# A two-layer encoder trunk on one core: output passes that start on half of their input, pools and allocations in another order, a norm on four columns

## The chip, the cores and the metric

The kernel runs on one core of a Trainium2 chip. The metric is device time in microseconds (us) of one execution; before the change the median of 3 runs is 1994.59 us (1993.06 to 1995.67). TensorE is PE here (its weight loads PEld), VectorE is DVE, ScalarE ACT, GpSimd POOL, and SP is the engine whose queue issues nearly all DMAs.

## The reference, cut to what matters

512 tokens of width 2048, all in float32. Layer A is a gated pooling mixer, then a key/value side is computed once, then layer B is latent attention.

```python
def pool_mixer_layer(x, norm_g, w_in, w_group, scale, w_out):      # layer A
    proj = rmsnorm(x, norm_g) @ w_in                  # 2048 -> 8192
    u, gate = proj[..., :W_A], proj[..., W_A:]        # 4096 each
    u = u.reshape(B, S, 4, 1024)                      # 4 groups, windows 2, 4, 8, 16
    pooled = stack([causal_mean_pool(u[:, :, g], w) - u[:, :, g] for g, w in ...])
    y = einsum('bsgc,gcd->bsgd', pooled, w_group) * scale
    return x + (y * silu(gate)) @ w_out               # 4096 -> 2048
...
h = rmsnorm(x, kv_norm_g); ckv = h @ kv_w_a; c = rmsnorm(c, kv_latent_g)   # shared k, v
...
proj = rmsnorm(x, norm_g) @ w_in                      # layer B: 512 latent + 2048 gate
q = rmsnorm(q_lat, q_latent_g) @ w_q_b                # 16 heads of 192
x + (attention(q, k, v) * silu(gate)) @ w_out
```

## The kernel before, in words

Activations lie with the feature on the partition and the 512 tokens along the row. A float32 product is three matmuls on rounded halves: hi times hi, hi times lo, lo times hi. "hi" is a cast on ACT, "lo" the difference, on DVE.

**Layer A, first pass (lines 384 to 431).** The 64 tiles of 128 columns of `awin` are made in 32 pairs. Each pair is computed by a seven-product scheme: for each of four quarters `q`, `w_combos` (269) loads 2 x 256 KB of weights into `raw`, DVE makes two sums (274), POOL two more (276, 277), ACT casts seven combinations to `hi` (280), DVE subtracts to `lo` (281). `seven` (291) then issues 21 matmuls of 256 columns for each of the two input blocks `j` of the quarter. A pair is 168 matmuls. `gather` (304) adds the pieces from PSUM. Pairs 0 to 15 are pooled (`pool_pair`, 318: log2(w) shifted adds, then a scale and a subtraction, then a store to `raws` in DRAM); pairs 16 to 31 are gates (`silu_pair`). The tuple `late` (402) is the order of the pairs. The norm of x is computed once in this pass (`norm_r`, 165): a matmul with a matrix of ones sums over the partitions, and the Newton steps of `rsqrt` (156) run on 128x512.

**Layer A, groups and output passes (433 to 487).** For b = 0 and 1: `group(2b, 0)` and `group(2b+1, 4)` multiply pooled groups by `awg`, eight accumulators each, all eight PSUM banks. At its end DVE multiplies each accumulator by scale and gate (457), then sums (463 to 465), ACT and DVE split them into the blocks `xh[j], xl[j]`: j = 0 to 3 from the first group, 4 to 7 from the second. The output pass then makes eight pairs of `awo`, each over q = 0 to 3, that is over j = 0 to 7 in order; b = 0 adds x, b = 1 adds the result of b = 0, and stores to `xres`.

**Layer B.** The pools of layer A are closed, and rpool, wpool, apool, bpool, xpool and tpool3 are opened in their place, at addresses in that order, from the lowest up. Each x tile is read back from `xres` (506), cast with the norm's gain (153, 154), and multiplied with `wkvc` into five accumulators. Then `norm_r` makes 1/rms of x, and DVE multiplies the accumulators by it (563, 566). Four latents (`proj` on `bwin`), two `latent_norm`, 16 gates, then eight units of two heads of attention, and the output projection.

A scheduler puts the instructions of each engine in order, and each engine runs its own list in that order; SP's list of DMAs too. A tile of a new pool waits for the last use of what lay at its address.

Of the kernel before, what the change touches and what calls it, by code (L numbers as in the profile page):

```python
# [51 lines left out]
def trunk_kernel(  # L52
# [111 lines left out]

    def norm_r(acc, n, p=None, r=None):

        p = tr() if p is None else p
        T.matmul(p, ones, acc, start=True, stop=True)
        v, a = (t[:, 0, 0:S] for t in (pt(), pt())) if r is not None else (tt_(), tt_())
        r = rpool.tile([P, S], F32, tag="r", name="r") if r is None else r  # L170
        V.tensor_scalar(v, p, 1.0 / n, EPS, ALU.mult, ALU.add)
        rsqrt(v, r, a, S)
        return r

# [59 lines left out]
    with ExitStack() as c1:  # L234
# [82 lines left out]

        def pool_pair(pair, v):

            w = WINS[pair // 4]  # L320
            up = pt()
            G.memset(up[:, :, 0:PAD], 0.0)
            V.tensor_tensor(halves(up[:, :, PAD:]), v, halves(r2), ALU.mult)
            prev, off = up, PAD
            m = 1
            while m < w:
                ext = w - 2 * m
                nw = S + ext
                nx = pt()
                V.tensor_tensor(nx[:, :, 0:nw], prev[:, :, off - ext:off + S],  # L330
                                prev[:, :, off - ext - m:off + S - m], ALU.add)
                prev, off = nx, ext
                m *= 2
# [67 lines left out]
        early = (18, 19, 20, 21)  # L401
        late = (22, 0, 23, 1, 2, 24, 3, 12, 25, 13, 26, 14, 27, 15, 28, 8, 29, 9, 30, 10, 11, 4, 5, 6, 7, 31)
        for n, pair in enumerate(early + late):
# [8 lines left out]
            if n == 4:  # L412
                V.tensor_tensor(sq[:, 0, :], sq[:, 0, :], sq[:, 1, :], ALU.add)
                p = ps7.tile([P, 2, H], F32, tag="k3", name="k3").rearrange("p h t -> p (h t)")
                norm_r(sq[:, 0, :], D, p, r2[:, 0, :])
                V.tensor_scalar(r2[:, 1, :], r2[:, 0, :], -1.0, None, ALU.mult)
            v = gather(ks)
            if n < 4:
                raws[pair] = dram()
                for m in range(2):  # L420
                    nc.sync.dma_start(raws[pair][:, m, :].rearrange("p (h t) -> p h t", h=2), v[:, m])
            elif pair < 16:
                pool_pair(pair, v)
                if pair < 6:
                    finish_gates(16 + pair)
            else:
                silu_pair(pair, halves(pt()[:, :, 0:S]), v, halves(r2))
# [4 lines left out]

        pp = c1.enter_context(tc.tile_pool(name="pp", bufs=2, **tile_))

        def group(g, j0):
# [14 lines left out]
            for o in range(8):  # L450
                if o % 2 == 0:
                    ys.append(pp.tile([P, 4, H], F32, tag="y", name="y", bufs=4))
                y = ys[-1][:, 2 - 2 * (o % 2):4 - 2 * (o % 2), :]
# [16 lines left out]
        for b in range(2):  # L470
            group(2 * b, 0)
            group(2 * b + 1, 4)
            for pair in range(NJ):
                ks = banks()
                for q in range(NJ // 2):
                    w = w_combos(*(awo[2 * b + q // 2, 2 * pair + m][:, (q % 2) * S:(q % 2 + 1) * S]
                                   for m in range(2)))
                    seven(ks, w, 2 * q)
                    seven(ks, w, 2 * q + 1)
                res = pp.tile([P, 2, S], F32, tag="y", name="y", bufs=4)  # L480
                nc.sync.dma_start(res, xres[pair] if b else xT[2 * pair:2 * pair + 2].rearrange("k p t -> p k t"))
                v = gather(ks)
                for m, op in enumerate((ALU.add, ALU.subtract)):
                    x = res[:, m, :].rearrange("p (h t) -> p h t", h=2)
                    V.tensor_tensor(x, x, v[:, m], op)
                xres[pair] = dram("xres", 16)
                nc.sync.dma_start(xres[pair], res)


    rpool = ctx.enter_context(tc.tile_pool(name="rpool", bufs=2, **tile_))  # L490
    wpool = ctx.enter_context(tc.tile_pool(name="wpool", bufs=3, **tile_))
    apool = ctx.enter_context(tc.tile_pool(name="apool", bufs=32, **tile_))
    bpool = ctx.enter_context(tc.tile_pool(name="bpool", bufs=32, **tile_))
    xpool = ctx.enter_context(tc.tile_pool(name="xpool", bufs=16, **tile_))
    tp[0] = ctx.enter_context(tc.tile_pool(name="tpool3", bufs=7, **tile_))
    ps = ctx.enter_context(tc.tile_pool(name="ps", bufs=2, space=bass.MemoryType.PSUM, **tile_))
# [46 lines left out]
    def latent_norm(lat, gcol):  # L543
        ac = tt_()
        A.activation(ac, lat[0], AF.Square)
        for o in range(1, 4):
            sq = tt_()
            A.activation(sq, lat[o], AF.Square)
            V.tensor_tensor(ac, ac, sq, ALU.add)
        r = norm_r(ac, 512)  # L550
        res = []
# [6 lines left out]

    rb[0] = norm_r(accs[0], D)
    cl = []  # L560
    for o in range(4):
        c = xt()
        V.tensor_tensor(c, kacc[o], rb[0], ALU.mult)  # L563
        cl.append(c)
    krT = tt_()
    V.tensor_tensor(krT, racc, rb[0], ALU.mult)
    pk = tr()
# [407 lines left out]
```

## Time and profile before

| | |
|---|---|
| median of 3 runs | 1994.59 us |
| the profiled execution | 1994.62 us, of which the span of the program is 1992.8 us |
| PE busy | 1914.0 us (96%) |
| PE weight loads | 1754.6 us (88%) |
| DVE busy | 1442.8 us (72%) |
| ACT busy | 848.6 us (43%) |
| POOL busy | 499.4 us (25%) |
| DMA | 254.53 MB, 128 GB/s over the span |
| mean granted clock of PE | 0.989 of full speed |

The stages of the profiled execution, in us from the start of the span: loading and first gates to about 60, the rest of the first pass to 685, groups of b = 0 to 764, its output pass to 942, groups of b = 1 to 1030, its output pass to 1212, the key/value input to 1276, latents and gates and the first unit's preparation to 1480, attention and output to 1993. PE is busy nearly throughout, so time can be lost only where PE is idle or runs at its lower clock: the view of PE's waits says for whom it waits, the timeline says when.

### The profile page before, as it was taken

To read this page: it belongs to the slowest core of one execution; us is meant where nothing else is said; L and a number is where in the kernel's file an instruction comes from. 1 tells how busy PE (TensorE), PEld (TensorE's weight loads), DVE (VectorE), ACT (ScalarE), POOL (GpSimd) and SP (SyncE) were. 2 spreads that over 40 slices of the span, in tenths; PEclk is the share of its full clock that TensorE was granted. 3 is DMA by queue.
4 is the path that set the end of the run, shared out by engine and by line. 5 is a ranking of instruction groups with operands and counts; after the bars stand their busy time and mean duration, and the time that the engine had idled before them with its cause. 6 is when DMAs were issued, how large, how long until landed. Compare 5 with 4: busy or idle time off the path is not lost.

```text
span 1992.8 us, 32684 instructions
## 1 busy us (share of the span) xinstructions
PE 1914.0 (96%) x12508; PEld 1754.6 (88%) x12508; DVE 1442.8 (72%) x2195; ACT 848.6 (43%) x1425; POOL 499.4 (25%) x516
## 2 busy tenths in 40 slices
PE   8999999999999997999998998899999999999999
PEld 7999999999999887999877997688888888888887
DVE  8779889999899867776576767674344788887322
ACT  7534333333333333333333335333243777785221
POOL 0434445555555205232033330000010111110000
PEclk9999999999999998999999998899999999999999
DMA  6644544334435563445544444222222111111632
GB/s 197 215 135 125 170 150 147 128 121 134 138 119 168 181 207 109 151 157 180 160 147 137 159 139 154 89 91 100 96 90 78 57 55 38 58 59 54 210 122 86
DMA packets 212046, 254.53 MB, mean 128 GB/s; under 512 B 14257, under 2 KB 155441, under 8 KB 211889
## 3 DMA queue, kind: packets, MB, share of 16 engines
q1 hardware_dynamic: 211600, 252.24, 39.1%
q8 instruction: 98, 1.61, 0.3%
q14 instruction: 60, 0.48, 0.1%
q10 hardware_dynamic: 288, 0.20, 0.0%
HBM read 219.88 MB, written 32.51 MB: 127 GB/s over the span
## 4 chain that ended last, share of the span: by engine, by line
PE 69%; DVE 15%; DMA 6%; issue 5%; ACT 4%; POOL 1%; SPq 1%; DVEq 0%; ACTq 0%; POOLq 0%
PE k L301 10%; PE k L299 10%; PE k L297 10%; PE mm L143 7%; PE mm L145 7%; PE mm L144 7%; DVE lo L281 5%; DMA raw<-awin 2%; PE k L143 2%; PE k L144 2%; PE k L145 2%; PE sc L766 2%; DMA raw<-awo 2%; PE mm L640 1%; PE mm L641 1%
## 5 line engine op out<-in xcount | busy, mean ns | idle before, releaser
L297 PE MATMUL k<-xh,hi 128*128 128x256 f32 x2576 | 706.0, 285 | 13.7 <-ACT xh L148 9.7
L299 PE MATMUL k<-xl,hi 128*128 128x256 f32 x2576 | 709.6, 285 | 3.2 <-DVE xl L149 3.2
L301 PE MATMUL k<-xh,lo 128*128 128x256 f32 x2576 | 648.9, 286 | 17.8 <-DVE lo L281 17.5
L280 ACT CAST hi<-raw 128x1792 fp32r<-128x1792 f32 x184 | 311.6, 1693 | 549.8 <-PE k L301 327.3
L297 PEld LDWEIGHTS k<-xh,hi 128*128 128x128 f32 x2576 | 495.3, 193 | 16.1 <-ACT xh L148 10.6
L299 PEld LDWEIGHTS k<-xl,hi 128*128 128x128 f32 x2576 | 498.2, 193 | 4.4 <-DVE xl L149 4.4
L281 DVE TENSOR_TENSOR lo<-raw,hi 128x1792 fp32r<-128x1792 f32 x184 | 405.9, 2207 | 108.2 <-ACT hi L280 107.7
L301 PEld LDWEIGHTS k<-xh,lo 128*128 128x128 f32 x2576 | 459.9, 193 | 23.1 <-DVE lo L281 22.5
L276 POOL TENSOR_TENSOR raw<-raw 128x256 f32<-128x256 f32 x184 | 218.6, 1188 | 728.6 <-DVE raw L274 656.6
L126 DVE TENSOR_TENSOR wlo<-raw,whi 128x512 fp32r<-128x512 f32 (+2 forms) x213 | 138.4, 656 | 178.3 <-ACT whi L125 177.2
L125 ACT CAST whi<-raw 128x512 fp32r<-128x512 f32 (+2 forms) x213 | 124.6, 596 | 272.0 <-PE mm L144 225.5
L277 POOL TENSOR_TENSOR raw<-raw 128x256 f32<-128x256 f32 x184 | 230.5, 1253 | 14.2
L274 DVE TENSOR_TENSOR raw<-raw 128x512 f32<-128x512 f32 x184 | 136.3, 741 | 47.0 <-DMA raw<-awo 25.5
L143 PE MATMUL mm<-bt,whi 128*128 128x512 f32 x348 | 137.5, 395 | 9.3 <-DVE xt L563 9.3
L145 PE MATMUL mm<-bt,wlo 128*128 128x512 f32 x348 | 137.0, 394 | 0.2 <-DVE wlo L126 0.2
L144 PE MATMUL mm<-bt,whi 128*128 128x512 f32 x348 | 136.5, 392 | 0.0
L144 PE MATMUL k<-lo,hi 128*128 128x512 f32 x256 | 99.6, 389 | 0.0
L145 PE MATMUL k<-hi,lo 128*128 128x512 f32 x256 | 99.6, 389 | 0.0
L149 DVE TENSOR_TENSOR lo<-raw,hi 128x1536 fp32r<-128x1536 f32 x32 | 56.0, 1756 | 54.7 <-ACT hi L148 50.8
L148 ACT CAST hi<-raw 128x1536 fp32r<-128x1536 f32 x32 | 47.2, 1482 | 96.1 <-PE k L145 60.4
L143 PEld LDWEIGHTS mm<-bt,whi 128*128 128x128 f32 x348 | 66.0, 190 | 24.2 <-issue 10.6
L145 PEld LDWEIGHTS mm<-bt,wlo 128*128 128x128 f32 x348 | 66.0, 190 | 14.7 <-DVE wlo L126 0.6
(815 smaller groups left out, 3064.1 us busy)
## 6 DMA issues: line engine op xcount, KB each, us to landing
raw<-awin SPq DMA_DIRECT2D x240, 256.0 KB, 3.2
raw<-awo SPq DMA_DIRECT2D x128, 256.0 KB, 3.1
raw<-bwin SPq DMA_DIRECT2D x80, 256.0 KB, 2.5
scr<-tp SPq DMA_DIRECT2D x32, 512.0 KB, 3.2
raw<-awg SPq DMA_DIRECT2D x32, 512.0 KB, 4.0
raw<-bwo SPq DMA_DIRECT2D x59, 256.0 KB, 2.6
raw<-scr SPq DMA_DIRECT2D x32, 256.0 KB, 4.3
y<-scr SPq DMA_DIRECT2D x32, 256.0 KB, 3.9
```

What stands on the lines that cost most here:

```text
L126: V.tensor_tensor(lo[:, :n], raw[:, :n], f(hi[:, :n]), ALU.subtract)
L143: T.matmul(dst, wh, xh, start=first, stop=False)
L144: T.matmul(dst, wh, xl, start=False, stop=False)
L145: T.matmul(dst, wl, xh, start=False, stop=last)
L274: V.tensor_tensor(c[:, :, 4:6, :], c[:, :, 0:1, :].broadcast_to([P, 2, 2, P]), c[:, :, 1:3, :], ALU.add)
L276: G.tensor_tensor(c[:, :, 6, :], c[:, :, 4, :], c[:, :, 2, :], ALU.add)
L277: G.tensor_tensor(c[:, :, 7, :], c[:, :, 6, :], c[:, :, 3, :], ALU.add)
L280: A.copy(hi, c[:, :, 1:8, :])
L281: V.tensor_tensor(lo, c[:, :, 1:8, :], f(hi), ALU.subtract)
L297: T.matmul(dst, hi[:, j % 2, wi, :], xh[j][:, xi, :], start=first, stop=False, skip_group_check=True)
L299: T.matmul(dst, hi[:, j % 2, wi, :], xl[j][:, xi, :], start=False, stop=False, skip_group_check=True)
L301: T.matmul(dst, lo[:, j % 2, wi, :], xh[j][:, xi, :], start=False, stop=last, skip_group_check=True)
```

## The change

Four parts.

1. **Output passes.** Each output pass issues quarters 0 and 1 of pairs 0 and 1 (the first group's half, j = 0 to 3) ahead of quarters 2 and 3 of pair 0. Pairs 2 to 7 are as before.
2. **Pools.** Layer B's pools are opened in the order rpool, wpool, tpool3, xpool, apool, bpool.
3. **Norm.** The sum over partitions is made with x as the weights and one column of ones as the stream, four times, so that it comes out with one token per partition, 128x4. `rsqrt` runs on 128x4. The four columns are spread on a diagonal (a 128x512 product with the identity), a matmul with ones brings them back to a row on every partition, ACT copies it out. Before the norm of layer B, ACT copies the five accumulators out of PSUM; the multiplications by 1/rms follow from there.
4. **Last group.** Pairs 12 to 15 (window 16) are only scaled and stored in the first pass, and pooled in the first output pass, after each odd pair, in `y` tiles of which there are four. The tuple `late` has another order.

```diff
+    def norm_r(acc, n, p, dg, outs):
+        for t in range(4):
+            T.matmul(p[:, t:t + 1], acc[:, t * P:(t + 1) * P], ones[:, 0:1], start=True, stop=True)
+        v, a, y = (spool.tile([P, 4], F32, tag=f"n{i}", name=f"n{i}", bufs=1) for i in range(3))
+        V.tensor_scalar(v, p[:, 0:4], 1.0 / n, EPS, ALU.mult, ALU.add)
+        rsqrt(v, y, a, 4)
+        V.tensor_tensor(dg.rearrange("p (t q) -> p t q", t=4), ident[:, None, :].broadcast_to([P, 4, P]),
+                        y[:, :, None].broadcast_to([P, 4, P]), ALU.mult)
+        T.matmul(p, ones, dg, start=True, stop=True)
+        for r, c in outs:
+            A.activation(r, p, AF.Copy, scale=c)
...
-        late = (22, 0, 23, 1, 2, 24, 3, 12, 25, 13, 26, 14, 27, 15, 28, 8, 29, 9, 30, 10, 11, 4, 5, 6, 7, 31)
+        late = (22, 0, 8, 23, 1, 9, 24, 2, 10, 25, 3, 11, 26, 4, 12, 27, 5, 13, 28, 6, 14, 29, 7, 15, 30, 31)
...
+            elif pair < 16:
+                z = pt()[:, :, 0:S]
+                V.tensor_tensor(halves(z), v, halves(r2), ALU.mult)
+                raws[pair] = dram()
+                nc.sync.dma_start(raws[pair], z)
...
+                if b == 0 and pair % 2:
+                    up = yp()
+                    nc.sync.dma_start(up[:, :, PAD:], raws[12 + pair // 2])
+                    pool_pair(12 + pair // 2, up, yp)
+            out_part(0, (0, 1))
+            out_part(1, (0, 1))
+            for pair in range(NJ):
+                out_part(pair, (2, 3) if pair < 2 else (0, 1, 2, 3))
+                out_end(pair)
...
     rpool = ctx.enter_context(tc.tile_pool(name="rpool", bufs=2, **tile_))
     wpool = ctx.enter_context(tc.tile_pool(name="wpool", bufs=3, **tile_))
+    tp[0] = ctx.enter_context(tc.tile_pool(name="tpool3", bufs=7, **tile_))
+    xpool = ctx.enter_context(tc.tile_pool(name="xpool", bufs=16, **tile_))
     apool = ctx.enter_context(tc.tile_pool(name="apool", bufs=32, **tile_))
     bpool = ctx.enter_context(tc.tile_pool(name="bpool", bufs=32, **tile_))
-    xpool = ctx.enter_context(tc.tile_pool(name="xpool", bufs=16, **tile_))
-    tp[0] = ctx.enter_context(tc.tile_pool(name="tpool3", bufs=7, **tile_))
...
-    rb[0] = norm_r(accs[0], D)
...
-        V.tensor_tensor(c, kacc[o], rb[0], ALU.mult)
+        A.copy(c, kacc[o])
         cl.append(c)
     krT = tt_()
-    V.tensor_tensor(krT, racc, rb[0], ALU.mult)
+    A.copy(krT, racc)
+    rb[0] = norm_r(accs[0], D, tr(), tt_(), [(r_tile(), 1.0)])
+    for c in cl:
+        V.tensor_tensor(c, c, rb[0], ALU.mult)
+    V.tensor_tensor(krT, krT, rb[0], ALU.mult)
```

The order of the instructions moves at these places. First, PE in the output pass of b = 0, where the second of pair 0's four weight blocks gives way to the next work. Before: after `hi_8231` (quarter 1 of pair 0) comes `hi_8283` (quarter 2 of pair 0) with `xh_8129`, the first block of the second group.

```order
L297 MATMUL k2_8171<-xh_7843,hi_8231 128x256
L299 MATMUL k2_8171<-xl_7844,hi_8231 128x256
L301 MATMUL k2_8171<-xh_7843,lo_8232 128x256
L297 MATMUL k0_8169<-xh_8129,hi_8283 128x256
L299 MATMUL k0_8169<-xl_8130,hi_8283 128x256
```

Now `hi_8251` is quarter 0 of pair 1, and `xh_7777` is a block of the first group; the second group's first block, `xh_8093`, follows 168 matmuls after the start of the pass, where it followed after 84.

```order
L308 MATMUL k2_8243<-xl_7778,hi_8251 128x256
L306 MATMUL k3_8244<-xh_7777,hi_8251 128x256
L308 MATMUL k3_8244<-xl_7778,hi_8251 128x256
L310 MATMUL k0_8133<-xh_7797,lo_8196 128x256
L310 MATMUL k1_8134<-xh_7797,lo_8196 128x256
```

Moved: two of pair 1's four weight blocks now stand ahead of the second group's half. DVE's list between the two groups' products and `xl` of the second group's second block holds five subtractions of line 281 (now 290) where it held three.

Second, SP's list at the end of the second output pass. Before, the first x tile of layer B (`tt__12418`) stands behind the store of the last pair:

```order
L487 DMA xres<-y 128x1024
L124 DMA raw<-wkvc 128x512 x3
L487 DMA xres<-y 128x1024
L506 DMA tt__12418<-xres 128x512
L124 DMA raw<-wkvc 128x512
L506 DMA tt__12472<-xres 128x512
```

Now three x tiles stand ahead of it; the first waits for PE alone (for the matmuls on the block that lay at its address):

```order
L512 DMA xres<-y 256x1x512
L542 DMA tt__12442<-xres 128x512
L124 DMA raw<-wkvc 128x512 x3
L542 DMA tt__12496<-xres 128x512
L542 DMA tt__12521<-xres 128x512
L512 DMA xres<-y 256x1x512
L124 DMA raw<-wkvc 128x512
```

Moved: three loads of 256 KB, from behind the last store to ahead of it.

Third, PE at the norm of layer B. Before, the matmul of the norm (L168), then the first latent, which waits for DVE to empty its bank:

```order
L523 MATMUL sc<-at,whi 64x512
L524 MATMUL sc<-at,whi 128x512
L168 MATMUL tr<-tt__12411,ones 128x512
L143 MATMUL mm<-bt,whi 128x512
L144 MATMUL mm<-bt,whi 128x512
```

Now four one-column matmuls, then the first latent, which waits for ACT's copy; the second matmul of the norm (L176 into `tr`) stands 40 matmuls further down.

```order
L559 MATMUL sc<-at,whi 64x512
L560 MATMUL sc<-at,whi 128x512
L170 MATMUL tr<-ones,tt__12435 128x1 x4
L143 MATMUL mm<-bt,whi 128x512
L144 MATMUL mm<-bt,whi 128x512
```

Moved: the Newton steps are no longer between the last product and the first latent on PE. From the first gate on, PE's list is as before.

## Rows read from the trace of the kernel before

**Rows 1.** Window of the first pass: length, then busy time of each engine (instructions), clock, DMA
```profile
core 0: us, PE busy (x) PEld busy (x) DVE busy (x) ACT busy (x) POOL busy (x), PEclk, DMA share, GB/s
60.00:685.00 625.00, 615.31 (x5048) 609.65 (x5047) 561.90 (x496) 236.60 (x175) 307.05 (x250) 1.00 0.46 148
```

**Rows 2.** PE's waits, whole span: us in total, times, longest us
```profile
PE k L301 <- DVE lo L281: 17.5, 20, 2.3
PE k L297 <- ACT xh L148: 9.7, 3, 5.3
```

**Rows 3.** Windows: openings (336 matmuls) of both output passes, parts, and what follows
```profile
764.50:800.40 35.90, 27.24 (x184) 25.79 (x185) 31.80 (x35) 13.78 (x12) 17.73 (x9) 0.86 0.37 119
764.50:821.10 56.60, 46.37 (x337) 44.33 (x338) 46.67 (x49) 20.81 (x17) 22.84 (x15) 0.91 0.40 128
821.10:941.90 120.80, 120.80 (x1009) 120.80 (x1009) 86.08 (x82) 42.01 (x30) 35.84 (x44) 1.00 0.51 165
1032.60:1071.00 38.40, 28.68 (x189) 27.21 (x190) 30.08 (x36) 13.69 (x12) 15.29 (x10) 0.87 0.39 123
1032.60:1091.10 58.50, 47.19 (x337) 45.12 (x338) 44.23 (x48) 20.72 (x17) 20.25 (x15) 0.91 0.38 123
```

**Rows 4.** Timeline of DVE in the openings: start, us, instruction, idle before
```profile
795.24 2.02 DVE L281 TENSOR_TENSOR lo<-raw,hi 128x1792 fp32r<-128x1792 f32 x1
...
799.16 1.22 DVE L149 TENSOR_TENSOR xl<-ts,xh 128x1024 fp32r<-128x1024 f32 x1 [1.11 <-ACT xh L148]
801.18 0.69 DVE L274 TENSOR_TENSOR raw<-raw 128x512 f32<-128x512 f32 x1 [0.80 <-DMA raw<-awo]
...
1069.80 1.22 DVE L149 TENSOR_TENSOR xl<-ts,xh 128x1024 fp32r<-128x1024 f32 x1
```

**Rows 5.** Timeline of POOL in the first opening
```profile
771.15 8.21 POOL L276 TENSOR_TENSOR raw<-raw 128x256 f32<-128x256 f32 x1 [6.08 <-DVE raw L274]
```

**Rows 6.** Timeline of all engines at the start of layer B
```profile
1212.20 0.37 ACT L308 COPY e<-k 128x256 f32<-128x256 f32 x1 [8.39 <-PE k L301]
...
1215.29 1.29 DVE L485 TENSOR_TENSOR y<-y,e 128x512 f32<-128x512 f32 x2
...
1217.03 0.38 SPq L506 DMA_DIRECT2D tt__12418<-xres  x1
...
1221.06 0.72 ACT L153 ACTIVATE at<-tt__12418,cs 128x512 fp32r<-128x512 f32 x1 [0.27 <-DMA tt__12418<-xres]
...
1221.83 1.23 PE L143 MATMUL mm<-at,xt 128*128 128x512 f32 x2 [9.67 <-ACT at L153]
```

**Rows 7.** Timeline of DVE and PE at the norm of layer B, and a window after
```profile
1276.82 0.68 DVE L171 TENSOR_SCALAR tt__12965<-tr 128x512 f32<-128x512 f32 x1
...
1285.71 0.76 PE L143 MATMUL mm<-bt,whi 128*128 128x512 f32 x1 [9.33 <-DVE xt L563]
...
1285.70:1291.60 5.90, 5.89 (x14) 4.64 (x15) 2.42 (x5) 0.62 (x1) 0.00 (x0) 0.50 0.01 3
```

**Rows 8.** Small work: a norm's weight loads, four transposes, a Newton step on eight columns
```profile
L168 PEld LDWEIGHTS tr<-tt__12411,ones x2: 188/188/189, 1275.1 to 1275.4; 128*128 128x128 f32 x2
...
1294.02 0.60 PE L569 MATMUL tr<-cs,tt__12988 128*128 128x128 f32 x4
1294.38 0.48 PE L143 MATMUL mm<-bt,whi 128*128 128x512 f32 x1
...
L163 DVE SCALAR_TENSOR_TENSOR sy<-sa,sy 128x8 f32<-128x8 f32 x22 | 4.0, 182 | 0.5
```

**Rows 9.** PE's waits from 320 to 470 (pools of window 16)
```profile
PE k L301 <- DVE lo L281: 3.1, 4, 1.0
```

**Rows 10.** PE's waits from 582 to 665 (five pools in a row)
```profile
PE k L301 <- DVE lo L281: 3.4, 4, 1.0
```

**Rows 11.** PE's waits from 240 to 300 (two pools in a row before)
```profile
PE k L301 <- DVE lo L281: 0.7, 1, 0.7
```

**Rows 12.** A group of DVE from 60 to 685: busy us, mean ns, idle before
```profile
L337 DVE SCALAR_TENSOR_TENSOR tp<-tp 128x1024 f32<-128x1024 f32 x16 | 24.3, 1517 | 0.2
```

More of the change, by code (lines that the diff above doesn't have):

```diff
@@ L163, in rsqrt, with r_tile @@
             V.scalar_tensor_tensor(y, a, 1.5, y, ALU.add, ALU.mult)
[L165 to L173, printed above, removed]
+    def norm_r(acc, n, p, dg, outs):
[9 more added lines that the diff above has]
+            A.activation(r, p, AF.Copy, scale=c)
+        return outs[0][0]
+    def r_tile():
+        return rpool.tile([P, S], F32, tag="r", name="r")
     post = const.tile([P, 4], I32, name="post")
@@ L316, in halves, with pool_pair @@
             return a.rearrange("p m (h t) -> p m h t", h=2)
-        def pool_pair(pair, v):
+        def pool_pair(pair, up, nt):
             w = WINS[pair // 4]
-            up = pt()
             G.memset(up[:, :, 0:PAD], 0.0)
-            V.tensor_tensor(halves(up[:, :, PAD:]), v, halves(r2), ALU.mult)
             prev, off = up, PAD
@@ L328, in pool_pair @@
                 nw = S + ext
-                nx = pt()
+                nx = nt()
                 V.tensor_tensor(nx[:, :, 0:nw], prev[:, :, off - ext:off + S],
@@ L414, in trunk_kernel @@
                 p = ps7.tile([P, 2, H], F32, tag="k3", name="k3").rearrange("p h t -> p (h t)")
-                norm_r(sq[:, 0, :], D, p, r2[:, 0, :])
-                V.tensor_scalar(r2[:, 1, :], r2[:, 0, :], -1.0, None, ALU.mult)
+                norm_r(sq[:, 0, :], D, p, pt()[:, 0, 0:S], [(r2[:, 0, :], 1.0), (r2[:, 1, :], -1.0)])
             v = gather(ks)
@@ L421, in trunk_kernel @@
                     nc.sync.dma_start(raws[pair][:, m, :].rearrange("p (h t) -> p h t", h=2), v[:, m])
-            elif pair < 16:
-                pool_pair(pair, v)
+            elif pair < 12:
+                up = pt()
+                V.tensor_tensor(halves(up[:, :, PAD:]), v, halves(r2), ALU.mult)
+                pool_pair(pair, up, pt)
                 if pair < 6:
                     finish_gates(16 + pair)
+            elif pair < 16:
[3 more added lines that the diff above has]
+                nc.sync.dma_start(raws[pair], z)
             else:
@@ L433, in trunk_kernel, with y_tile, yp @@
         pp = c1.enter_context(tc.tile_pool(name="pp", bufs=2, **tile_))
+        def y_tile():
+            return pp.tile([P, 2 * (PAD + S)], F32, tag="y", name="y", bufs=4)
+        def yp():
+            return y_tile().rearrange("p (m t) -> p m t", m=2)
         def group(g, j0):
@@ L451, in group @@
                 if o % 2 == 0:
-                    ys.append(pp.tile([P, 4, H], F32, tag="y", name="y", bufs=4))
+                    ys.append(y_tile()[:, 0:2 * S].rearrange("p (m t) -> p m t", m=4))
                 y = ys[-1][:, 2 - 2 * (o % 2):4 - 2 * (o % 2), :]
@@ L472, in trunk_kernel, with out_part, out_end @@
             group(2 * b + 1, 4)
-            for pair in range(NJ):
-                ks = banks()
-                for q in range(NJ // 2):
+            ks = {}
+            def out_part(pair, qs):
+                if qs[0] == 0:
+                    ks[pair] = banks()
+                for q in qs:
                     w = w_combos(*(awo[2 * b + q // 2, 2 * pair + m][:, (q % 2) * S:(q % 2 + 1) * S]
                                    for m in range(2)))
-                    seven(ks, w, 2 * q)
-                    seven(ks, w, 2 * q + 1)
-                res = pp.tile([P, 2, S], F32, tag="y", name="y", bufs=4)
+                    seven(ks[pair], w, 2 * q)
+                    seven(ks[pair], w, 2 * q + 1)
+            def out_end(pair):
+                res = yp()[:, :, 0:S]
                 nc.sync.dma_start(res, xres[pair] if b else xT[2 * pair:2 * pair + 2].rearrange("k p t -> p k t"))
-                v = gather(ks)
+                v = gather(ks.pop(pair))
                 for m, op in enumerate((ALU.add, ALU.subtract)):
@@ L549, in latent_norm @@
             V.tensor_tensor(ac, ac, sq, ALU.add)
-        r = norm_r(ac, 512)
+        r = norm_r(ac, 512, tr(), tt_(), [(r_tile(), 1.0)])
         res = []
```

## The prediction, written before the changed kernel was run

> **What bounds the kernel now.** The windows by stage come first. In the first pass PE is busy for 615.3 of 625 us at full clock [rows 1], and behind the opening of the first output pass it runs 1009 matmuls in 120.8 us without a gap, 0.12 us each [rows 3]. So PE is the bound nearly everywhere, and time can be won only where it stands still or runs slowly. PE's waits, read second, name those places: 17.5 us for the `lo` halves of DVE, 9.7 us for `xh` of ACT [rows 2]; the timelines add one stop at the start of layer B, 9.67 us, and one at its norm, 9.33 us [rows 6, 7]. The windows of the two openings, read third, are to be seen against the stretch behind them: 336 matmuls take 56.6 and 58.5 us where 336 times 0.12 is 40.3 [rows 3]. So 16.3 and 18.2 us are lost there, partly in stops, partly at a granted clock of 0.91. The profiled execution, 1994.62 us, is the base of the sum; the median of the runs, 1994.59, is the same within 0.03.
>
> **Openings of the output passes.** PE waits for the second group's blocks, which DVE and ACT make in a chain. DVE ends the last of them at 800.4 us (799.16 + 1.22) in the first opening and at 1071.0 in the second [rows 4]. Of the 336 matmuls only 184 and 189 have run by then [rows 3]; the rest take another 20.7 and 20.1 us. After the change the half of pair 1 that needs only the first group has been moved ahead, and by PE's order some 68 matmuls are left behind the last block: 8.2 us. Against that, DVE's list holds two more `lo` and three more sums ahead of that block (2 x 2.02 + 3 x 0.69 = 6.1 us, rows 4), and in the first opening also one add of a pool (1.5, the duration in rows 12): 7.6. DVE is idle for 4.1 of 35.9 us until its last block in the first opening, for 8.3 of 38.4 in the second [rows 3]. If all idle time is filled the last block is 3.5 us later in the first and no later in the second; if none, 7.6 and 6.1. Gain: 20.7 - 8.2 less 3.5 to 7.6 is 4.9 to 9.0, and 20.1 - 8.2 less 0 to 6.1 is 5.8 to 11.9. I take 8.0 and 9.5, towards the filled end, since the added work needs nothing of the second group. As outer bounds I keep nothing (the supply itself is the bound) and all that is lost, 16.3 and 18.2.
>
> **First pass.** The order of pairs changes where PE waits for `lo`. The pools of window 16 cost 3.1 us [rows 9] and five pools in a row 3.4 [rows 10]; both patterns go. In their place two pools and a gate follow each other at four places, and such a place costs 0.7 [rows 11], together 2.8; two of them have small windows, so I take 2.6. Gain 3.9; bounds 0 and 6.5.
>
> **The four last pools.** They move into the first output pass. Each is four adds and the final subtraction, 1.5 us each [rows 12], so some 7.5 us of DVE, 30 us in all. Behind the opening DVE is busy for 86.1 of 120.8 us [rows 3]; with the three pools that fall there it is about 109, 90% busy, as in the first pass, where that cost about 10 of 625 us [rows 1]. Each pool also loads 512 KB into a `y` tile on SP's queue, behind a store, and the first pool's add stands ahead of the second group's last block on DVE: if its load is late, that block is. I charge 1.5 us; bounds 0 and 6.
>
> **Start of layer B.** Before, DVE's sums of the last pair end with the add at 1215.29, then come the store, the load of x at 1217.03, ACT's cast of 0.72 at 1221.06, and PE at 1221.83 [rows 6]. PE loses 9.67 us and then, by the rate after the norm (0.42 us where 0.24 is full rate, rows 7), about 2.5 us at half clock: 12.2. Now three x tiles are loaded ahead of the last store, so that ACT can cast right behind its copy of the last pair: copy 0.37, cast 0.72 [rows 6], a square and `xt` of about 0.6 each, PE at about 1214.4. From there the first four blocks are paced by DVE, which still has gather and adds (some 4 us) in its list ahead of its `lo` halves. I leave 5 us lost: gain 7.2, bounds 2 and 10.
>
> **Norm of layer B.** The Newton chain runs from 1276.82 to PE's next matmul at 1285.71; PE stands 9.33 us, then makes 14 matmuls in 5.90 us at a granted clock of 0.50, the lower of the two levels, 1.2 GHz [rows 7]: 14 x (0.42 - 0.24) = 2.5 more. That is 11.8. After the change ACT's first copy releases the first latent's bank, and the steps on 128x4 take 11 x 0.18 = 2 us [rows 8] plus a product of 0.7; PE has 40 matmuls, 9.6 us, before the norm's second one. So PE waits for one copy at most. Gain 11.5; bounds 8 (DVE, held by its multiplications, is late with a weight half for the latents) and 11.8.
>
> **The norm's own matmuls.** A float32 matmul loads its weights twice (two loads of 0.188 us, rows 8); four one-column matmuls are eight loads, in four norms 32. Four transposes held PE for 0.36 us, 0.09 each [rows 8]. Between 0.09 and 0.188 a load this is 2.9 to 6.0 us. I take 2.9, since the transposes are the nearest whole instructions; as far as the columns hide behind other work it is less: bounds 1 and 6.
>
> **Rest.** From the first gate of layer B on, each engine has the same order; I take nothing there. The copies of the accumulators are five of ACT, some 3 us, hidden beside the first latent.
>
> **Sum.** 8.0 + 9.5 + 3.9 - 1.5 + 7.2 + 11.5 - 2.9 = 35.7 us; 1994.6 - 35.7 = 1958.9, in round figures 1959.
>
> **The rivals.** (1) The openings stay as long as they were, because what PE waits for is the supply of weight blocks and not the order. For it: POOL's sum of the third weight block took 8.21 us [rows 5], and the third block is needed after as many matmuls as before; in DVE's new list the second group's blocks stand behind `lo` halves that need POOL. Against it: the long waits for `xh` were 9.7 us of the whole span [rows 2], and they are what the new order puts off. Then 17.5 us of gain go: 1976.4. A page speaks for a milder form. The 8.21 us are longer than any single DVE instruction around them, the longest being 2.02 [rows 4]. The Trainium skill, "SBUF — State Buffer", section "Who interferes with whom", says that a DVE operation with two SBUF inputs and a POOL operation that reads SBUF exclude each other, and the loser is held until the other's instruction ends; the trace shows a hold across several instructions, not one. By the page's rule POOL would be done some 6 us sooner there and the opening less bound by supply; by the row a fuller DVE holds POOL longer. The measured row decides, and it is why I do not take the upper bound.
>
> (2) Slower. PE's stops in the openings do not go but are cut small: with work on both sides of each late block PE stops often and never long, and the clock stays at its lower level through both openings. At the rate of rows 7 (0.42 for 0.24) 336 matmuls take 70.6 us, 14.0 and 12.1 above before. Then the sum is 35.7 - 17.5 - 26.1 = -7.9: 2002.5. It decides only if the clock is low for most of the 40 us; with 0.91 before [rows 3], and fewer stops by the new order, little speaks for it. The Trainium skill, "TensorE: Matmul & The Clock Gate", section "HAM oscillation — how this bites in real kernels", says that work which comes in bursts between waits keeps dropping back to the slow clock. Here a stop of 9.33 us is followed by a clock of 0.50 [rows 7], and a mix of short stops by 0.91 [rows 3]; the trace bears it out only for the long one.
>
> (3) The change does not do what it says at the start of layer B: the loads of x, which now stand ahead in SP's list, wait for PE to leave the tiles' addresses, and weight loads stand behind them. Then the gain of 7.2 there is nothing: 1966.1.
>
> (4) The openings come near PE's own time: all 16.3 and 18.2 us come back, 17.0 more than in the sum: 1941.9.
>
> **How the numbers follow.** The forecast gets 0.58, rival 1 0.14, rival 3 0.15, rival 4 0.10, rival 2 0.03. Between the bounds of the terms the forecast reaches from about 1947 to 1972, rivals 1 and 3 lie at 1976 and 1966; from 1945 to 1977 the range leaves out rivals 4 and 2 and the forecast's edges, under 2 in 10. About 0.2%, 4 us, is what a measurement of this kernel can tell from no change; all cases but rival 2, and mishaps that add up, lie beyond it on the fast side: faster 0.94, same 0.02, slower 0.04.
>
> **What would show it.** Right: each opening's 336 matmuls take 47 to 50 us; PE's waits no longer list the casts of x in layer B and the product of the norm at over 9 us, and DVE's first x block of layer B follows the last pair's adds closely; waits for `lo` in the first pass fall by some 4 us; no stop appears in the first output pass. Wrong: openings still at 56 us or more with POOL's sums as long (rival 1); a clock under 0.7 in them (rival 2); the cast of x in layer B still behind the last store (rival 3); a new wait of PE behind a pool in the first output pass, or at the second matmul of a norm.

## The result, and the profile after

The changed kernel takes 1974.27 us (median of 4 runs, 1973.28 to 1975.29) beside 1993.82 for the kernel before (the median of 4 runs): a ratio of 0.9901, with a 95% interval of 0.9884 to 0.9918. All ratios below are times over the kernel before, with this interval in brackets. A second measurement on another occasion gave 0.9896 (0.9883 to 0.9908). It is faster by some 20 us. The forecast was 1959, the range 1945 to 1977: the sign and the range hold, the gain is a little over half of the 35.7 us in the sum. The time lies outside the forecast's own edges, 1947 to 1972, and close to the 1976.4 of rival 1, so the range held by the room that was left for the rivals.

The profiled execution has a span of 1971.5 us, 21.3 less than before. PE is busy for as long as before (1914.0 us), so what has gone is its idle time: 56.3 us where it was 78.8:

```profile
PE 1915.2 (97%) x12540; PEld 1753.3 (89%) x12540; DVE 1423.4 (72%) x2198; ACT 853.6 (43%) x1435; POOL 508.1 (26%) x516
```

PE's waits over the whole span, in us, times and longest (against [rows 2]; line 301 is now 310, 297 is 306, 281 is 290):

```profile
PE k L310 <- DVE lo L290: 13.1, 22, 1.2
...
PE k L308 <- DVE xl L149: 5.8, 3, 2.9
PE k L306 <- ACT hi L289: 4.3, 7, 0.8
PE mm L143 <- ACT xt L125: 2.1, 1, 2.1
...
PE k L306 <- ACT xh L148: 1.0, 2, 0.5
```

The stop of 9.33 us at the norm is gone, the one at the start of layer B is 2.1 where it was 9.67, and the waits for `xh` in the openings fell from 9.7 to 1.0 us. But two waits, mostly in the same openings, have taken part of their place: `xl` takes 5.8 us (3.2 before) and `hi` 4.3 (0.4 before).

Where the time went is read best by stages, cut at the first matmul of each; "layer B" starts at the end of the last matmul of the second output pass, so that its first stop lies in it. All runs of this study stand in the table (profiled execution, us); "first" reaches to the first group, "layer B" to the start of a run of 170 matmuls of the first unit's preparation that is the same in all (1486 us into the kernel before). The changed kernel stands there twice, and the two executions differ by up to 2.3 us in a stage. Other runs that share the order of every engine in a stage with it differ by more: 669.2 to 673.0 in the first pass (changed, r1, u1, u3, m1, d1), 177.6 to 181.0 in the first output pass (changed, r1, u3, n1, n2). So differences under some 3.5 us in these passes are not read. The groups of b = 1 (91.7 to 92.6 in runs with the changed order) and layer B (257.5 to 258.8 in runs with its three changes there) repeat within 1.3.

| run | first | groups b=0 | output b=0 | groups b=1 | output b=1 | layer B | rest |
|---|---|---|---|---|---|---|---|
| before | 674.7 | 89.8 | 177.5 | 90.6 | 179.5 | 273.9 | 506.8 |
| changed | 671.8 | 89.3 | 179.2 | 91.7 | 173.8 | 258.4 | 507.2 |
| changed again (r1) | 673.0 | 89.4 | 177.6 | 92.6 | 176.1 | 258.8 | 506.9 |
| u1 no early half of pair 1 | 671.2 | 89.2 | 181.2 | 92.0 | 179.1 | 258.1 | 508.0 |
| u2 pools and order undone | 679.2 | 89.6 | 173.5 | 89.3 | 175.2 | 257.6 | 507.6 |
| u3 old pool order in layer B | 670.8 | 89.2 | 181.0 | 92.0 | 176.8 | 264.5 | 507.7 |
| u4 old norm, no copies | 670.7 | 89.4 | 178.4 | 92.6 | 175.3 | 267.0 | 506.7 |
| m1 sums on DVE | 670.1 | 90.4 | 182.2 | 92.3 | 175.1 | 258.5 | 507.2 |
| m3 pools undone, new order | 678.0 | 89.4 | 173.7 | 89.8 | 174.7 | 257.5 | 506.8 |
| m6 m1 and m3 | 679.1 | 90.3 | 179.2 | 90.9 | 180.9 | 258.7 | 507.4 |
| n1 copies, wide norm | 667.1 | 89.5 | 179.1 | 92.6 | 174.8 | 254.8 | 506.6 |
| n2 the same again | 669.3 | 89.4 | 179.8 | 92.6 | 175.6 | 254.5 | 507.5 |
| b1 parts that paid | 675.0 | 89.2 | 174.0 | 89.8 | 174.7 | 254.7 | 507.8 |
| d1 DVE relieved | 669.2 | 89.0 | 184.5 | 92.5 | 176.2 | 258.5 | 507.6 |

Layer B gives 15.5 us of the 21.3 (15.1 by r1), the second output pass 5.7 (3.4 by r1), the first pass 2.9 (1.7 by r1); the rest loses 2.8 in the first of the two executions. The first output pass, for which the sum had 8.0 - 1.5, gives nothing: 177.5 before, 179.2 and 177.6 after.

The windows of the openings, with what [rows 3] show for before (columns as there; in each opening first the stretch to the end of the second group's last block, then all 336 matmuls, and between them what follows the first opening):

```profile
761.10:805.80 44.70, 38.41 (x283) 36.71 (x283) 38.40 (x41) 17.55 (x15) 24.67 (x16) 0.92 0.39 119
761.10:813.10 52.00, 45.12 (x336) 43.22 (x337) 43.95 (x46) 20.52 (x17) 25.21 (x16) 0.93 0.38 116
813.10:940.20 127.10, 123.26 (x1010) 121.38 (x1009) 114.77 (x106) 42.05 (x30) 52.89 (x47) 1.00 0.55 183
1032.00:1075.00 43.00, 36.65 (x279) 35.04 (x280) 37.32 (x40) 16.87 (x14) 25.53 (x15) 0.96 0.42 132
1032.00:1083.30 51.30, 44.11 (x337) 42.12 (x338) 42.30 (x44) 20.51 (x17) 26.08 (x15) 0.97 0.41 129
```

The openings take 52.0 and 51.3 us, for 56.6 and 58.5 (in r1 50.8 twice). Behind the last block PE needs 7.3 and 8.3 us, as the 8.2 of the working, though for 53 and 57 matmuls where the working had 68. But that block ends 44.7 and 43.0 us after the start, where it was 35.9 and 38.4: 8.8 and 4.6 later. And 1009 matmuls behind the first opening took 120.8 us before and take 127 now, with DVE busy for 114.8.

### The profile page after: what moved, and what is told of

It reads as the page before. It is cut to its first block, busy times and chain, and to the rows that moved or that the text cites. A ratio compares the mean times of both kernels' runs of the same rounds, so it can differ in the third digit from the quotient of the medians.

```text
span 1971.5 us, 32773 instructions
## 1 busy us (share of the span) xinstructions
PE 1915.2 (97%) x12540; PEld 1753.3 (89%) x12540; DVE 1423.4 (72%) x2198; ACT 853.6 (43%) x1435; POOL 508.1 (26%) x516
## 4 chain that ended last, share of the span: by engine, by line
PE 73%; DVE 10%; DMA 6%; issue 4%; ACT 4%; POOL 2%; SPq 0%; DVEq 0%; POOLq 0%; ACTq 0%
PE k L310 11%; PE k L308 10%; PE k L306 10%; PE mm L145 7%; PE mm L143 7%; PE mm L144 7%; DVE lo L290 4%; DMA raw<-awo 3%; PE k L143 2%; PE k L144 2%; PE k L145 2%; DMA raw<-awin 2%; PE sc L805 2%; PE mm L679 1%; POOL raw L285 1%
## 5 line engine op out<-in xcount | busy, mean ns | idle before, releaser
L285 POOL TENSOR_TENSOR raw<-raw 128x256 f32<-128x256 f32 x184 | 225.0, 1223 | 708.8 <-DVE raw L283 498.2
L286 POOL TENSOR_TENSOR raw<-raw 128x256 f32<-128x256 f32 x184 | 232.9, 1266 | 14.4
```

The source lines that it names most:

```text
L285: G.tensor_tensor(c[:, :, 6, :], c[:, :, 4, :], c[:, :, 2, :], ALU.add)
L286: G.tensor_tensor(c[:, :, 7, :], c[:, :, 6, :], c[:, :, 3, :], ALU.add)
```

## The experiments

**The early half of pair 1, undone (u1).**

```diff
-            out_part(0, (0, 1))
-            out_part(1, (0, 1))
             for pair in range(NJ):
-                out_part(pair, (2, 3) if pair < 2 else (0, 1, 2, 3))
+                out_part(pair, (0, 1, 2, 3))
                 out_end(pair)
```

> The changed kernel with each output pass issued pair by pair, as before; all else as changed. The sum of the prediction has 17.5 us in the two openings: then this run is 17.5 us slower than the changed kernel, near 1992. What the trace after the change shows of the openings (PE loses 12.5 and 13.6 us there where it lost 16.3 and 18.2, and the last block of the second group comes 44.6 and 42.9 us after the start) says about 9 to 11 us: 1983 to 1985. Rival: the early pair is worth nothing, since the supply of weight blocks bounds both orders: 1974.

Measured: 0.9942 (0.9925 to 0.9958), 1982.4 us. Against 0.9901 and 0.9896 the early half is worth 8 to 9 us, half of what the sum had; by the stages of the two output passes, 360.3 us here against 353.0 and 353.7, it is 7. By the windows above the openings of the changed kernel lose 11.7 and 11.0 us against 40.3, not the 12.5 and 13.6 of the expectation. The windows of the first output pass (opening, then the rest), and what follows the second opening in u1, in the changed kernel and in r1, tell more:

```profile
760.40:818.50 58.10, 45.34 (x337) 43.14 (x338) 48.41 (x50) 20.72 (x17) 22.83 (x16) 0.91 0.34 109
818.50:941.50 123.00, 121.59 (x1008) 120.99 (x1008) 112.81 (x102) 42.07 (x30) 57.54 (x47) 1.00 0.58 187
...
1091.60:1212.70 121.10, 121.10 (x1010) 120.97 (x1009) 84.57 (x81) 40.53 (x29) 37.51 (x44) 1.00 0.42 139
```

```profile
1083.30:1205.90 122.60, 121.35 (x1010) 120.95 (x1008) 88.55 (x85) 40.57 (x29) 38.30 (x44) 1.00 0.42 140
```

```profile
1083.40:1208.70 125.30, 123.05 (x1010) 122.55 (x1008) 87.43 (x85) 40.61 (x29) 36.48 (x44) 0.99 0.42 138
```

The opening alone is 6.1 us longer than in the changed kernel, but the rest is 4.1 shorter (123.0 against 127.1), though the same pools are computed there. A faster opening leaves DVE with more to do behind it. This is so behind the second opening too, where there are no pools: 121.1 us in u1, 122.6 in the changed kernel and 125.3 in r1. How the gain divides between the two passes is not shown: by the changed kernel the early half wins 2.0 us in the first output pass and 5.3 in the second, by r1 3.6 and 3.0.

**The last group's pools and the order of the pairs (u2, m3).** u2 puts the pools back into the first pass and restores the tuple `late`; m3 puts the pools back and keeps the new tuple.

```diff
-            elif pair < 12:
+            elif pair < 16:
                 up = pt()
...
-                if b == 0 and pair % 2:
-                    up = yp()
-                    nc.sync.dma_start(up[:, :, PAD:], raws[12 + pair // 2])
-                    pool_pair(12 + pair // 2, up, yp)
```

> The changed kernel with the last group pooled in the first pass and the pairs in their old order; all else as changed. The prediction has 3.9 us gained in the first pass and 1.5 lost in the output pass: this run 2.4 us slower, 1977. The trace after says that the output pass of b = 0 lost 5.4 us of PE to waits for lo behind its opening, where it lost none, and the opening there 2 us more than that of b = 1: this run then loses 4.3 in the first pass and wins 5.4 to 8 back, 1970 to 1973, with no wait of PE between the opening and the end of the first output pass.

> The changed kernel with the last group pooled in the first pass, at the places where the new order has its pairs; all else as changed. It parts the new order of the pairs from the move of the pools. Theory: the pools cost PE where they stand, about 1 us each in the first pass, and about 2 each in the first output pass and the group behind it: first pass 619 to 621 us (616.2 after, 623.9 with the old order), first output pass near 173.5 as without the pools, in all 3 to 5 us faster: 1969 to 1971. Rival: the first pass was shortened by the move alone and the order does nothing: 623.9 for the first pass, and the same time as the run with the old order, 1974.

Measured: u2 0.9895 (0.988 to 0.991), m3 0.9891 (0.9876 to 0.9906). Neither can be told from the changed kernel: this part of the change is worth nothing that these runs can tell. By stages the first pass is 5 to 8 us longer without the move, and the first output pass and the groups behind it 6 to 8 us shorter. The window behind the opening in m3:

```profile
819.10:940.90 121.80, 121.05 (x1009) 120.85 (x1008) 89.19 (x86) 41.99 (x30) 36.51 (x44) 1.00 0.52 170
```

Without the pools DVE is busy for 89.2 us there and PE loses almost nothing; with 25.6 us of pools more it takes 5.3 us longer. Another 1.9 to 2.4 lie in the groups of b = 1, whose first weight blocks wait behind the last pool. The order of the pairs does little by itself: 679.2 with the old, 678.0 with the new, and with the old norm 674.7 (before) and 675.0 (b1). PE's waits for `lo` in the first pass do fall with the order alone, from 11.3 us (u2) to 9.4 (m3) and from 9.4 (before) to 6.9 (b1), but no stage time is clear enough to show it. m3's rival holds, the order brings nothing that can be read there.

**Layer B's pools in their old order (u3).** The four lines that open tpool3, xpool, apool and bpool stand as before.

> The changed kernel with layer B's pools opened in their old order; all else as changed. The prediction has 7.2 us in this part: 1981.5. The trace after says about 4: PE still stops for 2.1 and 0.9 us at the start of layer B and runs 14 matmuls at the low clock, 8.4 us lost where it was 12.3: this run near 1978. Rival: the order of the pools does nothing, because the loads of x were not what the start waited for: 1974, and a first load of x ahead of the last store as in the changed kernel.

Measured: 0.9929 (0.9915 to 0.9944), and 6.1 us in the stage. The "about 4" of the expectation rested on a slip: the stop at the start of layer B had been counted in two neighbouring windows; with it counted once the changed kernel loses some 6 us there and not 8.4. In u3 the load stands behind the store again, and PE waits as it did before:

```profile
1214.29 0.52 SPq L512 DMA_DIRECT2D xres<-y  x1
1214.87 0.60 SPq L542 DMA_DIRECT2D tt__12442<-xres  x1
...
1219.47 1.65 PE L143 MATMUL mm<-at,xt 128*128 128x512 f32 x3 [9.63 <-ACT at L153]
```

In the changed kernel the load is issued 4.7 us before the last matmul of the pass starts (1205.63), and ACT casts right behind its copy. Two short stops of PE remain, behind ACT's in-order list (copy, cast, square, then the weights' cast) and behind DVE's gather. The clock falls at the end of the first of them, ahead of the first matmul of layer B, and is at 0.50, 1.2 GHz, for 6.5 us; the second stop lies in that stretch already (timeline of all engines, then windows):

```profile
1200.90 0.34 SPq L542 DMA_DIRECT2D tt__12442<-xres  x1
...
1205.94 0.37 ACT L317 COPY e<-k 128x256 f32<-128x256 f32 x1 [8.39 <-PE k L310]
1206.21 0.72 ACT L153 ACTIVATE at<-tt__12442,cs 128x512 fp32r<-128x512 f32 x1
...
1208.01 0.79 PE L143 MATMUL mm<-at,xt 128*128 128x512 f32 x1 [2.11 <-ACT xt L125]
...
1209.72 0.79 PE L144 MATMUL mm<-at,xt 128*128 128x512 f32 x1 [0.91 <-DVE at L154]
```

```profile
1205.90:1208.00 2.10, 0.01 (x1) 0.00 (x0) 1.51 (x3) 2.02 (x4) 0.00 (x0) 0.95 0.44 139
1208.00:1208.80 0.80, 0.79 (x1) 0.29 (x1) 0.77 (x2) 0.00 (x0) 0.00 (x0) 0.50 0.87 256
...
1208.00:1214.50 6.50, 5.58 (x12) 4.08 (x13) 6.46 (x11) 4.23 (x7) 0.00 (x0) 0.50 0.73 235
```

**The old norm and no copies (u4); copies with the old norm (n1, n2).** u4 restores `norm_r` and `rsqrt` on 128x512 in all four places and the multiplications out of PSUM; n1 and n2 restore the norm alone and keep these lines:

```diff
     for o in range(4):
         c = xt()
         A.copy(c, kacc[o])
         cl.append(c)
     krT = tt_()
     A.copy(krT, racc)
-    rb[0] = norm_r(accs[0], D, tr(), tt_(), [(r_tile(), 1.0)])
+    rb[0] = norm_r(accs[0], D)
     for c in cl:
         V.tensor_tensor(c, c, rb[0], ALU.mult)
```

> The changed kernel with the old norm in all four places and without the copies of the accumulators of layer B; all else as changed. The prediction has 11.5 us gained at the norm of layer B and 2.9 lost to one-column matmuls: this run 8.6 us slower, near 1983, with one stop of PE of over 9 us at the norm of layer B. The trace after shows 11.5 us gone from that place and little lost in the other norms (about 1 us): then 10.5 slower, near 1985. Rival: the gain is the copies' alone and the narrow norm costs more than it brings: not told apart by this run.

> The changed kernel with the old norm (128x512) in all four places, but with the copies of the accumulators of layer B by ACT. Theory: the copies release the first latent's bank and PE goes on; the Newton steps on 128x512, some 7.5 us on DVE, then only delay the weight halves of the latents by a little: no stop of over 9 us at the norm, time within 3 us of the changed kernel, 1974 to 1977. Rival: the stop only moves, since DVE is held by the steps and the latents' weights come late: near the run without copies, 1982.

> The changed kernel with the old 128x512 norm and ACT's copies of the accumulators, a second time. By stages it won 3.6 us over the changed kernel in layer B, where three norms no longer issue one-column matmuls, and 4.3 in the first pass, of which most must be chance if the narrow norm costs the same 1.2 us there. If so: 4 to 5 us under the changed kernel. If the first pass's share is real: 7 to 8.

Measured: u4 0.9935 (0.992 to 0.9949), with the old stop:

```profile
PE mm L143 <- DVE xt L591: 9.3, 1, 9.3
```

n1 0.9876 (0.9859 to 0.9894), n2 0.9871 (0.9859 to 0.9884): about 5 us faster than the changed kernel. Layer B takes 267.0 us with neither, 254.8 and 254.5 with the copies alone, 258.4 with copies and narrow norm. So the copies are worth 12.3 us and the narrow norm costs 3.6 to 4; DVE's Newton steps on 512 columns, now beside the first latent, hold nobody up. PE's rows show the price of the narrow norm. First the changed kernel, eight instructions for 0.80 us; then n1, two for 0.46:

```profile
1262.94 0.95 PE L170 MATMUL tr<-ones,tt__12435 128*128 128x1 f32 x8
...
1263.74 0.48 PE L143 MATMUL mm<-bt,whi 128*128 128x512 f32 x1
```

```profile
1259.50 1.02 PE L168 MATMUL tr<-tt__12427,ones 128*128 128x512 f32 x2
...
1259.96 0.79 PE L143 MATMUL mm<-bt,whi 128*128 128x512 f32 x1
```

The second matmul of the narrow norm takes as long as the only one of the wide norm, so 0.8 us are added in each norm, 2.4 in layer B's three; the other 1 to 2 us there are not accounted for. In the first pass, behind its one norm, the waits for `lo` from 160 to 300 us are 2.5 us in the changed kernel and 1.1 in n1 (first row the changed kernel, second n1). The runs with the narrow norm spread (1.2 in u1, 3.0 in r1), those with the wide one lie at 0.9 (u4, n2, b1); why a shorter DVE stretch goes with longer waits there is open.

```profile
PE k L310 <- DVE lo L290: 2.5, 5, 0.7
```

```profile
PE k L301 <- DVE lo L281: 1.1, 4, 0.4
```

**What bounds the openings (m1, m6, d1).** In the changed kernel's opening POOL's sum of the third block again takes 8.21 us, from 767.80 to 776.01, and DVE idles for 3.17 us until ACT can cast it:

```profile
767.80 8.21 POOL L285 TENSOR_TENSOR raw<-raw 128x256 f32<-128x256 f32 x1 [6.08 <-DVE raw L283]
```

```profile
774.73 0.69 DVE L283 TENSOR_TENSOR raw<-raw 128x512 f32<-128x512 f32 x1
778.58 2.03 DVE L290 TENSOR_TENSOR lo<-raw,hi 128x1792 fp32r<-128x1792 f32 x1 [3.17 <-ACT hi L289]
...
802.83 1.25 DVE L337 TENSOR_TENSOR y<-y 128x1052 f32<-128x1052 f32 x1
803.99 1.76 DVE L149 TENSOR_TENSOR xl<-ts,xh 128x1024 fp32r<-128x1024 f32 x1
```

m1 takes POOL out of it; m6 does so in m3.

```diff
-        def w_combos(a1, a2):
+        def w_combos(a1, a2, E=G):
...
-            G.tensor_tensor(c[:, :, 6, :], c[:, :, 4, :], c[:, :, 2, :], ALU.add)
-            G.tensor_tensor(c[:, :, 7, :], c[:, :, 6, :], c[:, :, 3, :], ALU.add)
+            E.tensor_tensor(c[:, :, 6, :], c[:, :, 4, :], c[:, :, 2, :], ALU.add)
+            E.tensor_tensor(c[:, :, 7, :], c[:, :, 6, :], c[:, :, 3, :], ALU.add)
...
-                                   for m in range(2)))
+                                   for m in range(2)), V if pair == 1 and q < 2 else G)
```

> The changed kernel with the two sums of pair 1's first two weight blocks made on DVE instead of POOL, in both output passes: four adds of 128x256 more on DVE in each opening, some 1.7 us. Theory: the openings now wait for POOL, whose sum of the third block takes 8.21 us while DVE is busy without a break, and for which DVE then stands idle for 3.2 us; with the sums on DVE the last block of the second group comes 3 to 5 us sooner in each opening and the kernel is 6 to 10 us faster: 1964 to 1968. Rival: DVE's own work bounds the openings, and 1.7 us more of it in each makes the kernel 0 to 4 us slower: 1974 to 1978.

> Both edits of the other two runs: the last group pooled in the first pass in the new order, and the sums of two weight blocks of each opening on DVE. If both theories hold the gains add up, 9 to 14 us below the changed kernel: 1960 to 1965. If only the first holds, 1969 to 1975.

Measured: m1 0.9911 (0.9896 to 0.9925), 1977.4 us, not faster; m6 0.9952 (0.9937 to 0.9967), 12 us slower than m3. The theory that POOL's sum bounds the openings falls. In m1 DVE no longer waits for that sum, but its list then stands three times for the loads of later blocks, and the last block comes 47.9 us after the start in the first opening and 43.8 in the second, where the theory had 40 to 42 (43.8 to 46.4 and 42.1 to 43.1 in the executions of changed, r1 and u3):

```profile
779.07 0.69 DVE L283 TENSOR_TENSOR raw<-raw 128x512 f32<-128x512 f32 x1 [1.15 <-DMA raw<-awo]
...
791.03 0.69 DVE L283 TENSOR_TENSOR raw<-raw 128x512 f32<-128x512 f32 x1 [1.73 <-DMA raw<-awo]
...
803.93 0.69 DVE L283 TENSOR_TENSOR raw<-raw 128x512 f32<-128x512 f32 x1 [1.97 <-DMA raw<-awo]
```

In m6 a wait that neither m1 nor m3 has, of PE for the gather of the first pairs, takes 6.1 us.

d1 takes DVE work out instead:

```diff
-                split(y[:, 0:3, :], xh[j][:, 0:3, :], xl[j][:, 0:3, :])
+                if j0:
+                    A.copy(xh[j][:, 0:3, :], y[:, 0:3, :])
+                    A.copy(xl[j][:, 0:3, :], y[:, 0:3, :])
+                else:
+                    split(y[:, 0:3, :], xh[j][:, 0:3, :], xl[j][:, 0:3, :])
```

> The changed kernel in which the lo part of the first three blocks of each tile of the second group is a copy by ACT instead of DVE's difference (so the values of these lo blocks are not the remainders): 3.8 us less of DVE in each opening, 3.3 more of ACT, nothing else. Theory: DVE's work ahead of the second group's last block, some 39 us, sets when it comes; the block comes 3 to 4 us sooner and each opening is shorter by as much: 6 to 8 us under the changed kernel. Rival: the chain of a weight block (load, DVE's sum, POOL's two, ACT's cast, DVE's difference) with its three buffers sets it: no change within 2 us, and DVE idles for longer instead.

Measured: 0.9918 (0.9905 to 0.993), 1978.7 us beside the 1974.9 of the changed kernel. Neither theory gave it. The stretch to the last block, in both openings:

```profile
758.20:802.00 43.80, 37.53 (x296) 36.31 (x297) 39.77 (x38) 21.61 (x19) 20.96 (x16) 0.99 0.39 121
1035.20:1077.10 41.90, 37.24 (x300) 36.26 (x301) 38.32 (x37) 21.51 (x19) 20.08 (x15) 1.00 0.45 139
```

With 3.8 us less to do for the second group DVE is as busy as ever (39.8 and 38.3 us), and the last block at most 1 us sooner (43.8 and 42.1 us after the start in r1): the scheduler put a seventh `lo` block ahead of the last block where the changed kernel has six. PE ran closer behind (296 and 300 matmuls by then, at a clock of 0.99 and 1.00), and lost it again in two waits for the gather,

```profile
PE k L306 <- DVE e L318: 6.7, 2, 3.6
```

as in m6. In all runs with the early half, DVE has 36 to 41 us of work ahead of the last block and stands idle for another 4 to 8. That points to its list as what sets the block's time, but it is not shown: in the idle time DVE stands for casts and loads, so the chain of a weight block, d1's rival, stays open, and d1 took no work out ahead of the block, since another `lo` came in its place. Whether a list that puts the group's blocks first would win was not tried.

**The parts that paid (b1).** Early half, new pool order, copies with the old norm, last group pooled in the first pass.

> The changed kernel itself, beside the next three on one chip, as the mark to measure them from: 0.990 of before, 1972 to 1976.

> The parts that paid: early half of pair 1, layer B's pools in the new order, ACT's copies with the wide norm, the new order of pairs; the last group pooled in the first pass as before. If the move of the pools costs 8 us in the first output pass and the group behind it and saves 5 in the first pass, this run is 2 to 3 us under the one with copies and wide norm, 1964 to 1967. Rival: the two places cost the same: equal to that run.

Measured side by side: r1 0.9896 (0.9883 to 0.9908), 1974.9 us; b1 0.9862 (0.9848 to 0.9876), 1967.7 us. b1 beats the changed kernel by 7 us and the kernel before by 28. Over n2 (1970.0) it is 2.3 us, inside the intervals.

## Why the prediction was right, and where its steps failed

The sign was right because the two large stops of layer B were real, could be read in one row each, and their cures worked: 12.3 and 6.1 us of the gain. Added up, the parts that the runs measured give 12.3 + 6.1 + 8 for the early half, nothing for the last group with the order of the pairs, less 5 for the narrow norm: 21 us, as measured. The sum's own arithmetic holds; its 0.24 us for a matmul at full rate is not in [rows 7] but twice the 0.12 of [rows 3]. Term by term:

- **Norm of layer B**, 11.5: right. u4 and n1 give 12.3 for the copies, a little over the upper bound of 11.8. But the forecast put part of it down to the small Newton chain; n1 shows that the copies do it alone.
- **Start of layer B**, 7.2: 6.1 by u3, inside its bounds; rival 3 is out, since the load does stand ahead of the store.
- **The norm's own matmuls**, -2.9: about -5 by the ratios of n1 and n2, inside its bounds. The 0.09 us of a transpose was a good price (0.10 each, 3.2 for all four norms). The rest is in no row: 1 to 2 us of it lie in layer B, and what the first pass adds is near the spread of its runs (669.2 to 673.0 us with the narrow norm, 667.1 to 670.7 with the wide one, the last group's pools moved in both).
- **First pass**, 3.9: the sum named the order of the pairs; the runs show the move of the pools (5 to 8 us in the stage) and for the order alone 2 to 2.5 us less waiting for `lo`, which no stage time shows. The sign that the term named did come: these waits fell from 9.4 us to 4.4. The four places of the new order are alike, each with a pool of window 2 and one of window 8, so the step from 2.8 to 2.6 had no ground.
- **The four last pools**, -1.5: mis-sized, the cost is 6 to 8 us. The step that failed is "with the three pools that fall there it is about 109, 90% busy, as in the first pass, where that cost about 10 of 625 us". The busy share came out as said (114.8 of 127.1), but a share did not set the price. A pool is some 7 us of DVE work that stands in DVE's list between the `lo` subtractions, in both places, and PE then waits for `lo`: 3.8 us in seven stops behind the first opening, where the sum had none and m3 has one of 0.8. Four pools cost 5 to 8 us in the first pass, and no less in the new place. The term should have been as large as the gain from taking them away.
- **Openings**, 17.5: mis-sized, 7 to 9 us by u1. The step that failed is "I take 8.0 and 9.5, towards the filled end, since the added work needs nothing of the second group". DVE's list is run in order, and the added `lo` blocks wait for casts and loads of their own: DVE idled for 6.3 us ahead of the last block in the first opening, 5.2 of them for casts, where it had idled for 4.1. The block came 8.8 and 4.6 us later, past the worst end of the first bracket (7.6), and the openings got 4.6 and 7.2 us shorter where the sum took 8.0 and 9.5. A second loss was in no term: what the opening wins is partly given back behind it, by u1 4.1 us behind the first opening and 1.5 behind the second (3.9 and 4.2 by r1). DVE has more left to do there; the pools are not the whole reason, since the second output pass has none.

Rival 1, that the supply is the bound, is out in the form that it gave, POOL's sum: taking that sum off POOL (m1) won nothing. That loads and casts bound the openings stays open. The rule in it from the Trainium skill, "SBUF — State Buffer", section "Who interferes with whom", by which the loser is held to the end of the other's instruction, is not borne out by the trace: the sum on POOL ended not behind one DVE instruction but at 776.0, 0.6 us after DVE's list paused, at 775.4, after eight instructions in a row. Rival 2 can be struck: the clock in the openings rose to 0.93 and 0.97 (1.00 and 0.93 in r1) with the fewer long stops. Its 0.91 before was a mean and no level: the clock was at 0.50 from 772.8 to 776.1 and from 786.5 to 793.2 us, around stops of 2.3 and 5.3 us, and at 1.00 between them. Rival 4 would have needed the last block some 32 us after the start, and DVE alone has 36 us of work or more ahead of it.

## What to carry to other kernels

When work is moved off a stop of the bound engine, price the engine that feeds it by its whole list ahead of the last item, idle time included, and follow the gain past the stage: a fed engine that catches up meets the next shortage. Work that cost the bound engine time in one stretch cost it about as much here in another in which its own engine was as busy, so price a move by the difference. And before narrowing a computation that sits on the path, look for the one thing that holds the path there: here a copy that freed a bank made the length of the computation irrelevant.

## What the runs showed of the hardware

A POOL add of 128x256, 0.74 us in the median, took 8.21 us in both openings of the kernel before and of the changed kernel (8.21 and 7.61 in r1); in the changed kernel's first opening DVE ran eight instructions without a pause beside it, and it ended 0.6 us behind the last of them. At the start of layer B the clock fell to 0.50 in a single stop of 2.1 us and stayed there for 6.5 us, with another stop of 0.9 in it; behind the first opening, with 3.8 us of waits in seven pieces of up to 1.2 us, it stayed at 1.00. Eight PE instructions for four one-column float32 matmuls took 0.80 us, 0.10 each.
